# Order of a few steps in a three-layer transformer kernel: where the score banks, row copies, weight splits and gated-attention stages stand in the queues

## The chip, the cores and the metric

The kernel runs on one core of a Trainium2 chip. A core has a matrix engine (TensorE, "PE" in the profile, its weight loads "PEld"), a vector engine (VectorE, "DVE"), an activation engine (ScalarE, "ACT"), GpSimdE ("POOL") and SyncE ("SP", which here only issues DMAs). The engines work their own queues in order and wait for one another by semaphores. The metric is the device time of one execution in microseconds (us), median of three runs.

## The reference, cut to what matters

256 tokens of width 1024 go through two layers of a first block (biased layer norms with modulation from a condition; layer 0 has differential attention, layer 1 multiscale pooling; both have a gated feed-forward) and one layer of a second block (gated linear attention and block attention with a distance bias side by side, then a feed-forward with a squared ReLU). All in float32.

```python
def swiglu(h, w_in, w_out):                     # feed-forward of layers 0 and 1
    g, u = jnp.split(h @ w_in, 2, axis=-1)
    return (jax.nn.silu(g) * u) @ w_out

# first block, end of each layer
x = layer_norm(ALPHA * x + g2 * swiglu(modulate(x, sh2, sc2), ffn_w_in[i], ffn_w_out[i]), ln_g[i, 1], ln_b[i, 1])

# second block
u = rms_norm(x, norm_mix) @ w_in
gq, gk, gv, g_lr, g_r, mq, mk, mv, gate_a, gate_b = jnp.split(u, points, axis=-1)
log_a = jax.nn.log_sigmoid(g_lr @ gla_gate_w2 + gla_gate_b) / GLA_GATE_TAU
o_a = gla_chunked(gq, gk, gv, log_a)            # chunks of 64 tokens, state carried from chunk to chunk
o_a = rms_norm(o_a, gla_out_norm) * jax.nn.silu(g_r)
sc = q @ k.T * scale - slopes * distance        # biased attention, softmax, times mv
y = jax.nn.sigmoid(gate_a) * (o_a @ w_branch_a) + jax.nn.sigmoid(gate_b) * (y_b @ w_branch_b)
x = x + y @ w_out
x = x + jnp.square(jax.nn.relu(rms_norm(x, norm_mlp) @ w_up)) @ w_down
```

## The kernel before

**Tiles.** The 256 tokens are two tiles t of 128. Every large product runs in split float32: an operand x is a rounded high part and a low part (x - high), and a product is three matmuls (high·high, high·low, low·high) in TensorE's fast float32 form. `mmN` (L376 to L378) multiplies tokens by a weight of 512 columns into one PSUM bank, `mmK` (L390, L392) one row block of a weight into two banks, `mmK_tail` (L403 to L405) the last blocks of an output, first half of the columns over all blocks, then the second half.

**Weights.** All weights come as blocks of 128x1024, in the order of a plan written by hand (`make_plan`). Class `Stream` loads them ahead on SP's queue (L255, eleven raw buffers). `emit` takes the next block: a weight is split, high part by ScalarE (L285) and low part by VectorE (L291), into one of eight buffer pairs; a modulation block "m" is a dot product on VectorE (L269). `get(key)` emits until that key is there; `done(keys)` frees a weight's buffers and calls `pump`, which emits up to seven blocks ahead of the last freed one (`R - SLACK`) and one modulation block a call. Where `done` or `get` stands in the program is where the splits stand in the queues of ScalarE and VectorE.

**PSUM.** Eight banks, three rings of two: "big" (two banks each), "mm" and "tr" (one bank each). A ring's next use waits until the use two before it has been read. `tr` serves transposes, `mm` projections, and in the biased attention also the scores.

**The feed-forward of layers 0 and 1** (`ffn`, L942) goes over six chunks j of the inner width: gate and up projections for both tiles, the hook `mid[j]`, then transposes `tr(j, t)` (L981) with their split (L425 on ScalarE into hh, L426 on VectorE into hl), and the output products `o(j - 1, t)` one chunk behind. In the last chunk the order is tr(5,0), o(4,0), tr(5,1), o(5,0), the norm of tile 0, then tile 1. In layer 0 hook 5 is `mid_gbr` (L1095): three calls of `col_row` (L767), which turns a column vector into a row on all partitions by 4 transposes (L774) and a ScalarE copy (L775) for each of two halves, in the tr ring; and `mod_cols` (L858), short VectorE operations on columns that need the modulation blocks. The rows are G and B of the coming norm, and `cur["grow"]`, by which `prescale` (L305) scales the pooling weights.

**The biased attention** (L1315 to L1360) runs between the twelve projections mv0 to gv1: `mo_s` makes scores (L1325, mm ring), bias, maximum and exponential; `mo_t` transposes them (tr ring); `mo_av` multiplies by mv. Two such steps follow each projection from the third on. A projection's result is copied from its bank by ScalarE (mv: L1377), behind the `done` of the weight in tile 1.

**The gated attention** (L1426 to L1507) runs between sixteen further products. Its stages are `g_z` (log gates la, by Abs, Exp and Ln on ScalarE and L1433 on VectorE), `g_b` (sums of la, L1438, and their exponentials), `g_kl` (L1447), `g_qk` (transposes L1455, scaled on VectorE), `g_a`, `g_kv(h)` (L1482, states on VectorE L1487 and L1489) and `g_o(t, h)`; all but g_o use the tr ring. The list `steps` gives one stage after a product, two after products 2 to 5.

**The last feed-forward** goes over eight chunks: `up` (with Relu L1595 on ScalarE and the square L1596 on VectorE), `trm` (transposes L1603), `down`.

Of the kernel before, what the change touches and what calls it, by code (L numbers as in the profile page):

```python
# [13 lines left out]
AF = mybir.ActivationFunctionType  # L14
# [157 lines left out]
def body(ctx: ExitStack, tc: tile.TileContext, wst, prm, cst, cst2, poolp, xT_d, cT_d, x_d, head, lam_d,  # L172
# [769 lines left out]
    def ffn(l, fp, x1_ready, after0, mid1, after1, mid):  # L942
        J = len(FFN_CHUNKS)
        ops_ = None
        hT = {}
        hs = {}

        def gu(j, t, which, ps, mid={}):
            c0, w = FFN_CHUNKS[j]
            n = D * w // (P * BW)  # L950
            lh = xlh(t)
            if is32((which, l, j)):
                lh = lambda k: xf[t, k // 4][:, k % 4]
            mmN(ps[:, :w], lh, mkey((which, l, j), n), width=w, mid=mid)

        def do_g(j, t):
            ps = mmt()
            gu(j, t, "G", ps)
            w = FFN_CHUNKS[j][1]
            h = fp.t([P, 512], f"h{t}", bufs=2)  # L960
            A.activation(h[:, :w], ps[:, :w], AF.Silu)  # L961
            hs[j, t] = h

        def do_u(j, t, mid={}):
            ps = mmt()
            gu(j, t, "U", ps, mid)
            w = FFN_CHUNKS[j][1]
            h = hs[j, t]
            V.tensor_tensor(h[:, :w], h[:, :w], ps[:, :w], op=OP.mult)

        def fin(j, which):
            c0, w = FFN_CHUNKS[j]
            st.done(*mkey((which, l, j), D * w // (P * BW)))

        def tr(j, t):
            w = FFN_CHUNKS[j][1]
            n = w // P
            h = hs.pop((j, t))
            ps = trt()
            for i in range(n):  # L980
                TE.transpose(ps[:, i * P:(i + 1) * P], h[:, i * P:(i + 1) * P], ident)  # L981
            hh = fp.t([P, 4, P], f"hh{t}", F32R, bufs=2)
            hl = fp.t([P, 4, P], f"hl{t}", F32R, bufs=2)
            pv = ps.rearrange("p (k t) -> p k t", t=P)[:, :n]
            split_evac(pv, hh[:, :n], hl[:, :n])
            hT[j, t] = (hh, hl)

        def o(j, t, done):
            n = FFN_CHUNKS[j][1] // P
            hh, hl = hT.pop((j, t))  # L990
            if j == J - 1:
                keys = [("O", l, j, i) for i in range(n)]
                mmK_tail(halves(ops_[t]), [(hh[:, i], hl[:, i]) for i in range(n)], keys)
                if done:
                    st.done(*keys[:HN[l]])
                    st.hold = True
                    st.done(*keys[HN[l]:])
                return
            for i in range(n):
                mmK(halves(ops_[t]), (hh[:, i], hl[:, i]), ("O", l, j, i), j == 0 and i == 0, False)  # L1000
                if done:
                    st.done(("O", l, j, i))

        for j in range(J):
            if j == 0:
                do_g(0, 0)
                do_u(0, 0, {XR[l]: x1_ready})
                if XR[l] == 8:
                    x1_ready()
                do_g(0, 1)  # L1010
                fin(0, "G")
                do_u(0, 1)
                fin(0, "U")
                ops_ = [big(), big()]
            else:
                do_g(j, 0)
                if j == 1:
                    tr(0, 1)
                do_g(j, 1)
                fin(j, "G")  # L1020
                do_u(j, 0)
                do_u(j, 1)
                fin(j, "U")
            if j in mid:
                mid[j]()
            if j < J - 1:
                if j > 0:
                    o(j - 1, 0, False)
                tr(j, 0)
                if j > 0:  # L1030
                    o(j - 1, 1, True)
                    tr(j, 1)
            else:
                tr(j, 0)
                o(j - 1, 0, False)
                tr(j, 1)
                o(j, 0, False)
                if l == 0:
                    for b in range(2):
                        st.prescale(("PW", b))  # L1040
                after0(ops_[0])
                if l == 0:
                    st.hold = True
                o(j - 1, 1, True)
                mid1()
                o(j, 1, True)
                after1(ops_[1])
                if l == 1:
                    st.hold = False
                    st.pump()  # L1050
# [42 lines left out]
        nx["g1p"] = g1p  # L1093

    def mid_gbr():  # L1095
        nx["G"], nx["B"] = col_row(nx["gb"][0]), col_row(nx["gb"][1])
        cur["grow"] = col_row(nx["g1p"])
        nx["cols"] = mod_cols(1, 1, 2)

    mrs = {}  # L1100
    pb = []
# [35 lines left out]
        for f in range(2):  # L1137
            A.activation(pw[t][:, f * 512:(f + 1) * 512], pst[f], AF.Copy)

    ffn(0, fp, x_t(1), ac0(0), mid_pool, ac0(1), {XM: mid_xa, 2: mid_g2c, 3: mid_g2r, 4: mid_gb, 5: mid_gbr})  # L1140


    pps = [big()]
# [171 lines left out]
    def mo_s(t, g):  # L1315
        nh, nk = (4, 128) if t == 0 else (2, 256)
        if g == 0:
            mo_sum[t] = small(8)
        ps = mmt()
        sc = mo.t([P, 512], "sc", bufs=2)  # L1320
        mx = small(4)
        dd = c2c("d0") if t == 0 else c2c("d1")
        for j in range(nh):
            h = nh * g + j
            TE.matmul(ps[:, j * nk:(j + 1) * nk], qT[:, h, t * P:(t + 1) * P], kT2[:, h, 0:nk], start=True, stop=True)  # L1325
        for j in range(nh):
            h = nh * g + j
            sl = slice(j * nk, (j + 1) * nk)
            V.scalar_tensor_tensor(sc[:, sl], dd, 2.0 ** -(h + 1), ps[:, sl], op0=OP.mult, op1=OP.add)
        V.tensor_reduce(mx[:, :nh], sc.rearrange("p (h k) -> p h k", k=nk), AX.X, OP.max, negate=True)  # L1330
        for j in range(nh):
            h = nh * g + j
            sl = slice(j * nk, (j + 1) * nk)
            A.activation(sc[:, sl], sc[:, sl], AF.Exp, bias=mx[:, j:j + 1], accum_out=mo_sum[t][:, h:h + 1])
        mo_st[t, g] = sc
# [36 lines left out]
    seq = [(c, t) for c in ("mv0", "mv1", "gq", "gk", "gv0", "gv1") for t in range(2)]  # L1372
    per = -(-len(steps) // 9)
    for i, (c, t) in enumerate(seq):
        ps = proj(c, t, t == 1)
        if c[:2] == "mv":
            A.activation(mv[:, t, 512 * int(c[2]):512 * int(c[2]) + 512], ps, AF.Copy)  # L1377
        elif c == "gq":
            A.activation(gq[:, t], ps, AF.Copy)
        elif c == "gk":  # L1380
            A.activation(gk[:, t], ps, AF.Copy)
        else:
            A.activation(gv[:, t, 512 * int(c[2]):512 * int(c[2]) + 512], ps, AF.Copy)
        while qk_wait:
            qk_tr()
        if i >= 2:
            for _ in range(per):
                if steps:
                    steps.pop(0)()
# [113 lines left out]
    def g_fin(t):  # L1503
# [5 lines left out]
        for h in range(GH):  # L1509
# [4 lines left out]
    tr_evac(s[1], 1, *obT)  # L1514
    seq = [("gb0", 0), ("gb0", 1), ("gb1", 0), ("gb1", 1), ("bb0", 0), ("bb0", 1), ("bb1", 0), ("bb1", 1),
           ("ga0", 0), ("ga0", 1), ("ga1", 0), ("ga1", 1), ("gr0", 0), ("gr1", 0), ("gr0", 1), ("gr1", 1)]
    steps = [lambda: (g_z(0), g_z(1)), lambda: g_b(0), lambda: g_b(1), lambda: (g_kl(0), g_kl(1)), lambda: g_qk(0), lambda: g_qk(1),
             lambda: g_a(0), lambda: g_a(1), lambda: g_kv(0), lambda: g_kv(1), lambda: (g_o(0, 0), g_o(1, 0)), lambda: g_kv(2),
             lambda: (g_o(0, 1), g_o(1, 1)), lambda: g_kv(3), lambda: (g_o(0, 2), g_o(1, 2)),
             lambda: (g_o(0, 3), g_o(1, 3))]  # L1520

    def oblh(t):
        return lambda k: (obT[0][:, k, t * P:(t + 1) * P], obT[1][:, k, t * P:(t + 1) * P])
# [1 line left out]
    for i, (c, t) in enumerate(seq):  # L1525
# [13 lines left out]
        else:  # L1539
# [5 lines left out]
            else:  # L1545
# [1 line left out]
                A.activation(e, ps, AF.Tanh, scale=0.5)  # L1547
                V.scalar_tensor_tensor(gs[t][:, sl], e, 1.0, ps, op0=OP.add, op1=OP.mult)
                V.tensor_tensor(gs[t][:, sl], gs[t][:, sl], gon[:, sl], op=OP.mult)
        for _ in range(1 + (1 < i < 6)):  # L1550
            if steps:
                steps.pop(0)()
        if (c, t) == ("gr1", 0):
            while steps:
                steps.pop(0)()
            g_fin(0)
    g_fin(1)

# [30 lines left out]
    def up(j, t, mid={}):  # L1589
        ps = mmt()  # L1590
        mmN(ps, xlh(t), mkey(("UP", j), 4), mid=mid)
        if t == 1:
            st.done(*mkey(("UP", j), 4))
        h = fp.t([P, 512], f"h{t}", bufs=2)
        A.activation(h, ps, AF.Relu)  # L1595
        V.tensor_tensor(h, h, h, op=OP.mult)  # L1596
        hs[j, t] = h

    def trm(j, t):
# [30 lines left out]
    for j in range(1, J):  # L1630
        up(j, 0)
        up(j, 1)
        if j < J - 1:
            down(j - 1, 0, False)
            trm(j, 0)
            down(j - 1, 1, True)
            trm(j, 1)
        else:
            trm(j, 0)
            down(j - 1, 0, False)  # L1640
            trm(j, 1)
            down(j, 0, False)
            rcore(0)(ops_[0])
            down(j - 1, 1, True)
            rx_t(0, prmc("nple"))
            down(j, 1, True)
            rcore(1)(ops_[1])
# [122 lines left out]
```

## Time and profile before

| | us |
|---|---|
| median of 3 runs | 1158.18 (1155.91 to 1158.88) |
| the profiled execution | 1158.82 |
| its span, first to last instruction | 1156.8 |
| TensorE / VectorE / ScalarE busy | 1116.0 / 760.6 / 558.8 |

The profile is that of one execution. Its page gives busy shares and the costliest groups of instructions by line; further views of the same trace list who waited for whom, single instructions in order of time, and busy time and granted clock by stretch. A row of a timeline is start, duration, engine, line, operation, output<-inputs by the program's names, forms and count, and in square brackets the idle time before it and who ended it. Rows of several like instructions are merged (x8). Matmuls overlap their neighbours, so distances from start to start say more of TensorE than durations. The granted clock is 1.00 (2.4 GHz) or 0.50 (1.2 GHz).

### The profile page before, as it was taken

How to read it: one execution, taken by the hardware profiler on the slowest of the kernel's cores; microseconds unless marked ns; L12 is line 12 of the kernel's file. 1: busy time of each engine (PE TensorE's matmuls, PEld its weight loads, DVE VectorE, ACT ScalarE, POOL GpSimd, SP SyncE). 2: the span in 40 equal slices, each digit the busy share in tenths (PEclk: the TensorE clock that was granted, in tenths of full speed). 3: DMA queues.
4: the chain of work that ended last, by engine and by line, in shares of the span. 5: the costliest groups of instructions: out<-in, count | busy, mean ns of one | idle time of the engine just before them, and what ended most of it. 6: DMA issues, size and time to landing. Idle time of an engine off the chain costs nothing. (4 is left out here: it accounts for less than half of the span.)

```text
span 1156.8 us, 14163 instructions
## 1 busy us (share of the span) xinstructions
PE 1116.0 (96%) x5186; PEld 881.8 (76%) x5186; DVE 760.6 (66%) x1114; ACT 558.8 (48%) x913; POOL 22.7 (2%) x35
## 2 busy tenths in 40 slices
PE   7999888999999999999999999999999999999998
PEld 3578665678888776888887787886777877888887
DVE  7984967669986875677346765455545785555465
ACT  3452456454444527544444755457235374445353
POOL 0000000000000000000000110000000000000000
PEclk9999989999999999999999999999999999999999
DMA  9972742569997915668563755444344645464611
GB/s 360 351 274 102 273 145 66 196 236 357 354 419 286 336 58 203 218 225 300 170 231 119 241 188 180 146 164 153 102 146 130 216 151 195 166 210 163 206 38 37
DMA packets 65922, 234.62 MB, mean 203 GB/s; under 512 B 7323, under 2 KB 8347, under 8 KB 65852
## 3 DMA queue, kind: packets, MB, share of 16 engines
q1 hardware_dynamic: 64080, 227.97, 55.7%
q10 hardware_dynamic: 1772, 5.74, 1.5%
q8 instruction: 41, 0.67, 0.2%
q14 instruction: 29, 0.24, 0.1%
HBM read 232.63 MB, written 1.05 MB: 202 GB/s over the span
## 5 line engine op out<-in xcount | busy, mean ns | idle before, releaser
L291 DVE TENSOR_TENSOR lo<-raw,hi 128x1024 fp32r<-128x1024 f32 x316 | 375.2, 1220 | 139.8 <-ACT hi L285 136.1
L285 ACT ACTIVATE hi<-raw 128x1024 fp32r<-128x1024 f32 x316 | 322.5, 1056 | 82.9 <-PE mm L378 60.9
L376 PE MATMUL mm<-hi,xTh 128*128 128x512 f32 (+1 forms) x872 | 337.6, 387 | 4.0 <-ACT xTh L425 2.7
L377 PE MATMUL mm<-lo,xTh 128*128 128x512 f32 (+1 forms) x872 | 331.8, 380 | 2.0 <-DVE lo L291 1.3
L378 PE MATMUL mm<-hi,xTl 128*128 128x512 f32 (+1 forms) x872 | 332.2, 381 | 0.6 <-DVE xTl L738 0.4
L376 PEld LDWEIGHTS mm<-hi,xTh 128*128 128x128 f32 x872 | 164.1, 188 | 40.8 <-issue 4.7
L378 PEld LDWEIGHTS mm<-hi,xTl 128*128 128x128 f32 x872 | 164.0, 188 | 34.0 <-DVE xTl L426 1.9
L377 PEld LDWEIGHTS mm<-lo,xTh 128*128 128x128 f32 x872 | 164.2, 188 | 33.5 <-DVE lo L291 3.6
L269 DVE SCALAR_TENSOR_TENSOR raw<-raw,crow 128x1024 f32<-128x1024 f32 x80 | 96.7, 1218 | 0.0
L390 PE MATMUL big<-hi,hh 128*128 128x512 f32 x256 | 80.6, 396 | 0.0
L390 PE MATMUL big<-lo,hh 128*128 128x512 f32 x256 | 79.2, 391 | 0.0
L392 PE MATMUL big<-hi,hl 128*128 128x512 f32 x256 | 79.0, 390 | 0.0
L425 ACT ACTIVATE hh<-tr 128x512 fp32r<-128x512 f32 (+1 forms) x40 | 23.0, 576 | 97.4 <-PE tr L981 54.8
L961 ACT ACTIVATE h<-mm 128x512 f32<-128x512 f32 (+1 forms) x24 | 13.5, 561 | 90.2 <-PE mm L378 90.2
L426 DVE TENSOR_TENSOR hl<-tr,hh 128x512 fp32r<-128x512 f32 (+1 forms) x40 | 26.3, 661 | 46.3 <-ACT hh L425 45.6
L392 PEld LDWEIGHTS big<-hi,hl 128*128 128x128 f32 x256 | 48.1, 188 | 10.4
L390 PEld LDWEIGHTS big<-lo,hh 128*128 128x128 f32 x256 | 48.0, 188 | 10.3
L390 PEld LDWEIGHTS big<-hi,hh 128*128 128x128 f32 x256 | 46.7, 188 | 8.6
L420 POOL TENSOR_TENSOR st<-st,half 128x4 f32<-128x4 f32 (+1 forms) x28 | 21.8, 778 | 1036.8 <-DVE st L418 1023.6
L1596 DVE TENSOR_TENSOR h<-h 128x512 f32<-128x512 f32 x16 | 11.0, 688 | 33.6 <-ACT h L1595 33.5
L1595 ACT ACTIVATE h<-mm 128x512 f32<-128x512 f32 x16 | 9.6, 599 | 38.0 <-PE mm L378 38.0
L667 ACT ACTIVATE p<-big,st 128x512 f32<-128x512 f32 x16 | 11.0, 689 | 31.7 <-DVE st L666 31.7
(316 smaller groups left out, 1261.5 us busy)
## 6 DMA issues: line engine op xcount, KB each, us to landing
raw<-in_dram SPq DMA_DIRECT2D x426, 512.0 KB, 5.0
row<-in_dram ACTq DMA_DIRECT2D x8, 512.0 KB, 6.4
tok<-in_dram SPq DMA_DIRECT2D x8, 256.0 KB, 7.5
xa<-in_dram SPq DMA_DIRECT2D x2, 512.0 KB, 5.7
out_dram<-sg SPq DMA_DIRECT2D x3, 256.0 KB, 2.0
pmat<-in_dram ACTq DMA_DIRECT2D x1, 544.0 KB
crow<-in_dram ACTq DMA_DIRECT2D x1, 512.0 KB, 6.8
out_dram<-sg SPq DMA_DIRECT2D x2, 128.0 KB, 1.7
```

What stands on the lines that cost most here:

```text
L269: V.scalar_tensor_tensor(raw, raw, 1.0, crow, op0=OP.mult, op1=OP.mult, accum_out=mc[l][:, nb:nb + 1])
L285: A.activation(hi, raw, AF.Copy)
L291: V.tensor_tensor(lo, raw, hi.bitcast(F32), op=OP.subtract)
L376: TE.matmul(ps, h, hi[:, sl], start=s, stop=False)
L377: TE.matmul(ps, h, lo[:, sl], start=False, stop=False)
L378: TE.matmul(ps, l, hi[:, sl], start=False, stop=e)
L390: TE.matmul(halves[f], h, w[:, f * 512:(f + 1) * 512], start=first and b == 0, stop=False)
L392: TE.matmul(halves[f], l, hi[:, f * 512:(f + 1) * 512], start=False, stop=last)
L420: G.tensor_tensor(r, v, half_e[:, :w], op=OP.pow)
L425: A.activation(dh, ps, AF.Copy)
L426: V.tensor_tensor(dl, ps, dh.bitcast(F32), op=OP.subtract)
L961: A.activation(h[:, :w], ps[:, :w], AF.Silu)
```

## The change

Six edits of order; no computation is added or left out.

1. `ffn`, last chunk, layer 1: `st.get` of the chunk's last output block stands right behind the transposes of tile 0, where before it was fetched when the product came to it. The same in the last feed-forward for the block ("DN", 7, 3).
2. `ffn`, last chunk: two new hooks, `mid[j, 0]` behind the transposes of tile 0 and `mid[j, 1]` behind o(j - 1, 0). In layer 0 the row B is made in the first and the row for `prescale` in the second; `mid_gbr` keeps G and the columns.
3. The scores of the biased attention take a tr bank and not an mm bank.
4. For mv, `done` in tile 1 stands behind the copy of the bank.
5. The gated attention has eleven steps and not sixteen, one after each of the first eleven products: g_z; g_b of both tiles; g_kl; g_qk(0); g_qk(1); g_a of both; g_kv(0); then for each head both g_o and the next g_kv.
6. The first `up` of tile 1 calls `done` behind Relu and square.

```diff
@@ ffn, last chunk
                 tr(j, 0)
+                if l == 1:
+                    st.get(("O", l, j, FFN_CHUNKS[j][1] // P - 1))
+                if (j, 0) in mid:
+                    mid[j, 0]()
                 o(j - 1, 0, False)
+                if (j, 1) in mid:
+                    mid[j, 1]()
                 tr(j, 1)
                 o(j, 0, False)
@@ hooks of layer 0
     def mid_gbr():
-        nx["G"], nx["B"] = col_row(nx["gb"][0]), col_row(nx["gb"][1])
+        nx["G"] = col_row(nx["gb"][0])
+        nx["cols"] = mod_cols(1, 1, 2)
+
+    def mid_br():
+        nx["B"] = col_row(nx["gb"][1])
+
+    def mid_pr():
         cur["grow"] = col_row(nx["g1p"])
-        nx["cols"] = mod_cols(1, 1, 2)
...
-    ffn(0, ..., {..., 4: mid_gb, 5: mid_gbr})
+    ffn(0, ..., {..., 4: mid_gb, 5: mid_gbr, (5, 0): mid_br, (5, 1): mid_pr})
@@ mo_s
-        ps = mmt()
+        ps = trt()
@@ projections beside the biased attention
-        ps = proj(c, t, t == 1)
-        if c[:2] == "mv":
-            A.activation(mv[:, t, 512 * int(c[2]):512 * int(c[2]) + 512], ps, AF.Copy)
...
+        ps = proj(c, t, t == 1 and c[:2] != "mv")
...
+        A.activation(dst, ps, AF.Copy)
+        if t == 1 and c[:2] == "mv":
+            st.done(*mkey((c,), 4))
@@ steps of the gated attention
-    steps = [lambda: (g_z(0), g_z(1)), lambda: g_b(0), lambda: g_b(1), lambda: (g_kl(0), g_kl(1)), lambda: g_qk(0), lambda: g_qk(1),
-             lambda: g_a(0), lambda: g_a(1), lambda: g_kv(0), lambda: g_kv(1), lambda: (g_o(0, 0), g_o(1, 0)), lambda: g_kv(2),
-             lambda: (g_o(0, 1), g_o(1, 1)), lambda: g_kv(3), lambda: (g_o(0, 2), g_o(1, 2)),
-             lambda: (g_o(0, 3), g_o(1, 3))]
+    steps = [lambda: (g_z(0), g_z(1)), lambda: (g_b(0), g_b(1)), lambda: (g_kl(0), g_kl(1)), lambda: g_qk(0),
+             lambda: g_qk(1), lambda: (g_a(0), g_a(1)), lambda: g_kv(0)]
+    for h in range(GH):
+        def head(h=h):
+            g_o(0, h)
+            g_o(1, h)
+            if h < GH - 1:
+                g_kv(h + 1)
+        steps.append(head)
...
-        for _ in range(1 + (1 < i < 6)):
-            if steps:
-                steps.pop(0)()
+        for f_ in steps[i:i + 1]:
+            f_()
@@ up, last feed-forward
-        if t == 1:
+        if t == 1 and j:
             st.done(*mkey(("UP", j), 4))
         h = fp.t([P, 512], f"h{t}", bufs=2)
         A.activation(h, ps, AF.Relu)
         V.tensor_tensor(h, h, h, op=OP.mult)
+        if t == 1 and not j:
+            st.done(*mkey(("UP", j), 4))
@@ its last chunk
             trm(j, 0)
+            st.get(("DN", j, 3))
             down(j - 1, 0, False)
```

## Rows read from the trace of the kernel before

**Rows 1.** Page, busy us (share of the span), instructions.

```profile
PE 1116.0 (96%) x5186; PEld 881.8 (76%) x5186; DVE 760.6 (66%) x1114; ACT 558.8 (48%) x913; POOL 22.7 (2%) x35
```

**Rows 2.** Waits of TensorE: line, who ended it: us in total, times, longest.

```profile
PE big L404 <- DVE lo L291: 1.8, 3, 0.6
...
PE tr L1603 <- DVE h L1596: 1.3, 1, 1.3
...
PE tr L1447 <- ACT gtmp L1441: 0.9, 2, 0.6
PE tr L1455 <- DVE qkd L1459: 0.8, 1, 0.8
...
PE tr L774 <- ACT row L775: 0.4, 2, 0.3
PE tr L981 <- ACT row L775: 0.4, 2, 0.2
```

**Rows 3.** Timeline of TensorE, end of layer 0's feed-forward (start, us, engine, line).

```profile
392.64 1.03 PE L774 MATMUL tr<-cst,Gc 128*128 128x128 f32 x8
393.92 1.14 PE L774 MATMUL tr<-cst,Bc 128*128 128x128 f32 x8 [0.25 <-ACT row L775]
...
396.60 0.66 PE L981 MATMUL tr<-cst,h 128*128 128x128 f32 x4 [0.20 <-ACT row L775]
...
402.58 0.60 PE L981 MATMUL tr<-cst,h 128*128 128x128 f32 x4
```

**Rows 4.** Timeline of ScalarE in the same stretch.

```profile
393.27 1.09 ACT L775 ACTIVATE row<-tr 128x512 f32<-128x512 f32 x2 [0.39 <-PE tr L774]
```

**Rows 5.** Timeline of VectorE there, first and last of an unbroken run.

```profile
393.44 1.22 DVE L291 TENSOR_TENSOR lo<-raw,hi 128x1024 fp32r<-128x1024 f32 x1
...
402.05 0.68 DVE L426 TENSOR_TENSOR hl<-tr,hh 128x512 fp32r<-128x512 f32 x1
```

**Rows 6.** Timeline of TensorE, two waits that a lower clock followed.

```profile
160.11 1.09 PE L681 MATMUL tr<-cst,p 128*128 128x128 f32 x4 [3.68 <-DVE st L707]
...
823.41 1.55 PE L1482 MATMUL tr<-gv,gk 64*128 64x256 f32 x6 [1.44 <-DVE gst L1489]
```

**Rows 7.** Stretches: us, busy (x) PE, PEld, DVE, ACT, POOL; clock; DMA.

```profile
158.60:165.40 6.80, 5.29 (x20) 3.75 (x20) 4.80 (x11) 5.06 (x15) 0.32 (x1) 0.50 0.68 240
...
824.20:827.50 3.30, 3.30 (x10) 2.17 (x9) 1.39 (x3) 0.00 (x0) 0.00 (x0) 0.50 0.38 151
```

**Rows 8.** Timeline of TensorE, last output blocks of the last feed-forward.

```profile
1112.58 0.39 PE L405 MATMUL big<-hi,hl 128*128 128x512 f32 x1
1112.80 0.39 PE L403 MATMUL big<-hi,hh 128*128 128x512 f32 x1
1113.79 0.50 PE L404 MATMUL big<-lo,hh 128*128 128x512 f32 x1 [0.59 <-DVE lo L291]
```

**Rows 9.** Timeline of ScalarE ahead of it.

```profile
1110.93 0.60 ACT L425 ACTIVATE hh<-tr 128x512 fp32r<-128x512 f32 x1 [5.28 <-PE tr L1603]
```

**Rows 10.** Timeline of TensorE, a projection beside the biased attention.

```profile
717.24 0.50 PE L376 MATMUL mm<-hi,xTh 128*128 128x512 f32 x1 [1.17 <-ACT mv L1377]
```

**Rows 11.** Timeline of ScalarE ahead of it.

```profile
712.82 3.88 ACT L285 ACTIVATE hi<-raw 128x1024 fp32r<-128x1024 f32 x4
716.61 0.57 ACT L1377 ACTIVATE mv<-mm 128x512 f32<-128x512 f32 x1
```

**Rows 12.** Timeline of TensorE, first matmul behind g_b(0).

```profile
790.01 0.48 PE L376 MATMUL mm<-hi,xTh 128*128 128x512 f32 x1
```

**Rows 13.** Timeline of VectorE, la of tile 1.

```profile
790.49 0.69 DVE L1433 SCALAR_TENSOR_TENSOR la<-tr,gtmp 128x512 f32<-128x512 f32 x1 [3.68 <-ACT gtmp L1432]
```

**Rows 14.** Timeline of ScalarE in g_z, first of three table loads.

```profile
784.15 1.28 ACT L1432 ACT_TABLE_LOAD   x1
```

**Rows 15.** Page, groups: out<-in xcount, busy us, mean ns, idle before, releaser.

```profile
L1596 DVE TENSOR_TENSOR h<-h 128x512 f32<-128x512 f32 x16 | 11.0, 688 | 33.6 <-ACT h L1595 33.5
L1595 ACT ACTIVATE h<-mm 128x512 f32<-128x512 f32 x16 | 9.6, 599 | 38.0 <-PE mm L378 38.0
```

More of the change, by code (lines that the diff above doesn't have):

```diff
@@ L1138, in ple @@
             A.activation(pw[t][:, f * 512:(f + 1) * 512], pst[f], AF.Copy)
-    ffn(0, fp, x_t(1), ac0(0), mid_pool, ac0(1), {XM: mid_xa, 2: mid_g2c, 3: mid_g2r, 4: mid_gb, 5: mid_gbr})
+    ffn(0, fp, x_t(1), ac0(0), mid_pool, ac0(1), {XM: mid_xa, 2: mid_g2c, 3: mid_g2r, 4: mid_gb, 5: mid_gbr, (5, 0): mid_br, (5, 1): mid_pr})
     pps = [big()]
@@ L1374, in body @@
     for i, (c, t) in enumerate(seq):
-        ps = proj(c, t, t == 1)
-        if c[:2] == "mv":
-            A.activation(mv[:, t, 512 * int(c[2]):512 * int(c[2]) + 512], ps, AF.Copy)
[L1378 to L1383, printed above, removed]
+        ps = proj(c, t, t == 1 and c[:2] != "mv")
+        dst = dict(mv=mv, gv=gv, gq=gq, gk=gk)[c[:2]][:, t]
+        if c[2:]:
+            dst = dst[:, 512 * int(c[2]):512 * int(c[2]) + 512]
+        A.activation(dst, ps, AF.Copy)
+        if t == 1 and c[:2] == "mv":
+            st.done(*mkey((c,), 4))
         while qk_wait:
@@ L1549, in body @@
                 V.tensor_tensor(gs[t][:, sl], gs[t][:, sl], gon[:, sl], op=OP.mult)
-        for _ in range(1 + (1 < i < 6)):
-            if steps:
-                steps.pop(0)()
+        for f_ in steps[i:i + 1]:
+            f_()
         if (c, t) == ("gr1", 0):
-            while steps:
-                steps.pop(0)()
             g_fin(0)
```

## Prediction

> **What bounds the kernel now.** I read the page's busy shares first: TensorE is busy for 1116.0 of the 1156.8 us of the span [rows 1]. So a change of order is worth what it does to the 40 us in which TensorE stands still, and I went on to the list of TensorE's waits. The waits with names that this change touches are short: 1.8 us in three places for a low part of an output block, 0.9 and 0.8 us in the gated attention, 1.3 us for a squared activation, and 0.4 + 0.4 us for the row copies of the first feed-forward [rows 2]. Then I read the timeline of each place on three engines, to see what a moved step gets in front of it. TensorE, ScalarE and VectorE work their queues in order, so each moved step carries its waits to all that is behind it.
>
> **Row copies between the last blocks of the first feed-forward: a cost.** This edit decides the result. Name the bank uses of the tr ring: before, G1 G2 B1 B2 P1 P2 (two halves of three rows), then T0 = tr(5,0), then o(4,0), then T1 = tr(5,1). The ring has two banks, so each use waits until the one two before it has been read out: B1 starts at 393.92 [rows 3], just after the copy of G1, half of the 1.09 us from 393.27, has ended [rows 4]. After: G1 G2 T0 B1 B2, o(4,0), P1 P2 T1. B2 now takes the bank of T0, and T0's last reader is not ScalarE but VectorE, the subtraction that writes hl. In the trace this hl starts at 402.05 and takes 0.68 us [rows 5]. It can't come sooner in the changed kernel: VectorE runs without a gap from 393.44 to 402.05 [rows 5], four low parts and three modulation dot products of 1.22 us each, which overlap a little, and five short column operations, and all of these were queued by fin(5, "U") and mid_gbr, which still stand ahead of T0. (The columns of mod_cols, moved up within mid_gbr, are those five; their place in VectorE's queue is the same.) In the kernel before nobody minds, since TensorE passes from T0 at 396.60 straight to o(4,0), which fills the time up to T1 at 402.58 [rows 3]. In the changed kernel o(4,0) is queued behind B2, so the cover stands behind the wait.
>
> The sum. Four transposes of a half take about 0.44 us (the copy of G1 starts 0.63 after the first one [rows 3, 4], some 0.2 of it hand-over). T0 starts at 393.92, B1 at about 394.46, when G2's copy has ended, and is through at 394.90. B2 waits until hl ends at 402.73, so it starts at 402.83: TensorE idles for 7.9 us. Then 0.44 for B2, o(4,0) with 402.58 - 396.60 - 0.44 = 5.54 us [rows 3], and P1, P2 and the refill wait of T1, 1.28 us as from G to B now [rows 3]: T1 at 402.83 + 0.44 + 5.54 + 1.28 = 410.09 against 402.58, **+7.5 us**. After it everything keeps its distances to T1, so nothing gives this back: prescale needs P's row, which is copied before T1, and the 0.6 us for the last low part stays, since the early fetch is for layer 1 alone.
>
> To this comes the clock. The trace has a wait of 3.68 us that ends at 160.11 [rows 6], and around it the granted clock is 0.50, the 1.2 GHz level, up to 165.40, that is for 5.3 us after work resumed; after a wait of 1.44 us that ends at 823.41 [rows 6] it is 0.50 for 3.4 us [rows 7]. At half speed half of that time is lost: 2.65 or 1.7 us. A wait of 7.9 us can hardly get less; I take 2.2, between the two. The edit: **+9.7 us** (9.2 to 10.2; 7.5 if the clock stayed up).
>
> **Last output blocks fetched early (layer 1, and the last feed-forward).** In mmK_tail the first half uses all four blocks; the fourth block's low part isn't there, and the matmul at 1112.80 is followed by one at 1113.79, where neighbours stand 0.22 to 0.23 apart [rows 8]: 0.76 us, and 0.1 behind it for the refilled pipeline. Fetched right after the first transposes, the high part on ScalarE and the low part on VectorE go into a stretch in which ScalarE is idle for 5.28 us [rows 9], and the next copy there (hh of the other tile) still finds it done. The fetch moves one raw-block DMA on SP's queue forward too; that queue waits for nothing else here. Twice 0.85: **-1.7 us** (-1.2 to -1.75).
>
> **Scores in the tr banks, value copies ahead of the next splits.** Both aim at one wait. At 717.24 a projection waits 1.17 us [rows 10] for its mm bank, which the copy of mv releases, and this copy, at 716.61, is queued behind four high-part splits of 3.88 us [rows 11]. With the scores out of the mm ring the projection takes a bank that was read one projection earlier; with done behind the copy the copy goes first. Either is enough, so their gains aren't added. Some 0.3 us go beside it, where a projection now waits for a score bank. The four splits of each done move behind the copy, 0.6 us, and the next projection reaches its fourth block some 4 us later, so this is covered. In the tr ring a score bank is refilled by the next scores or transposes only after a projection of 5.5 us, longer than its reading by VectorE; if that cover failed the wait would return under another name. **-1.5 us** (0 to -1.9).
>
> **Gated attention.** Four terms. (1) g_kv(1) no longer follows g_kv(0): the wait that ends at 823.41 [rows 6] goes, 1.5 us, and the 3.4 us at clock 0.50 after it [rows 7], worth 1.7. (2) g_qk(1) gets a projection ahead of it: the wait of 0.8 [rows 2] goes, with the refill 0.95. (3) g_kl after a whole projection: 0.9 [rows 2]. (4) Against it, g_b(1) now comes right after g_b(0), which ends at 790.01 [rows 12], but la of tile 1 is written from 790.49 to 791.18 [rows 13]: a new wait of 1.2 us with the whole next projection queued behind it. Its source, the logarithms and exponentials of g_z on ScalarE, keeps its place. Sum 1.5 + 1.7 + 0.95 + 0.9 - 1.2: **-3.9 us** (-1.5 to -4.5). No later stage has less than a projection between writer and reader.
>
> The three exchanges of tables in g_z cost 1.28 us each by the trace [rows 14]. The Trainium skill (ScalarE: Activation LUTs, section Table sets: the hidden batching unit) says that one set holds both exp and ln, so that they need a single load. By that rule la of tile 1 would come two loads sooner and term (4) would vanish, which is 1.2 us less in the sum, 1159.3; here the trace shows the loads between them, so the row decides.
>
> **Square ahead of done in the last feed-forward.** TensorE waits 1.3 us for the square [rows 2], but Relu (599 ns) and square (688 ns) follow one another whatever stands around them [rows 15]; with only one low part out of the way I take **-0.2 us** (0 to -0.4). The four splits come later by that much and have a projection in front of them.
>
> **How the numbers follow.** +9.7 - 1.7 - 1.5 - 3.9 - 0.2 = +2.4 us. The profiled execution took 1158.82 us (span 1156.8 and 2.0 around it), so 1161.2 by it; that execution is 0.64 above the median of the three runs, 1158.18, so against the median 1160.5. What a measurement of this kernel can tell from no change is about 0.3%, 3.5 us. **Forecast: no change that can be told, 1160.5** (its own range 1158 to 1161.6), the stall in the first feed-forward eating all the other gains: chance 0.61.
>
> **Rivals.** *The clock makes it slower.* The new 1.2 us wait in the gated attention lies between a wait of 1.17 us without a fall of the clock and one of 1.44 with one [rows 10, 6, 7]. If the clock falls there too the 1.7 us of term (1) aren't won, and with 2.65 us lost behind the long wait the sum is +2.4 + 1.7 + 0.45 = +4.6: 1162.7. It decides from the point at which the granted clock shows 0.50 behind g_b. With scores that merely change the name of their wait (the change doing not what it says, +1.5) it is 1164. For it: one fall in the trace followed a wait of 1.44 us; against: the wait at 717 had none. Chance 0.24.
>
> *The row copies are free and it is faster.* If B2's bank were free when it is wanted, the edit would cost nothing and win some of the 0.8 us of row waits, and the other terms would stand: -7.3 to -8, so 1150.5. For it: no row of the kernel before shows a wait of TensorE for hl. Against: hl has seven long operations in front of it in a queue that is worked in order, and the rings' refills are seen to wait for readers on ScalarE and VectorE alike [rows 3, 6]. Chance 0.15, the rest of the doubt about my reading of the queue among it.
>
> From these: faster by over 0.3% 0.15, within 0.3% 0.61, slower by over 0.3% 0.24. The range reaches from 1156 to 1164: the faster case lies outside, the slower one inside.
>
> **What would show it.** In the profile after: transposes of Bc (L774) with an idle time of about 8 us released by VectorE's hl, ahead of o(4,0) at about 403, and a clock of 0.50 behind it; no wait for lo at the tails of layer 1 and of the last feed-forward, one still in layer 0; no wait of a projection for mv; none of g_kv for gst; a new one of about 1.2 us of g_b for la. If the long stall isn't there, the forecast is wrong by its largest term.

## The result: faster by 0.7%, since the long stall wasn't there

The changed kernel takes 1148.99 us (median of four, 1148.72 to 1149.45) against 1157.05 of the kernel before; the ratio is 0.9929, 95% interval 0.9912 to 0.9947. The forecast was 1160.5, no change that can be told. Faster had a chance of 0.15.

The page of the changed kernel has 6 us less of busy TensorE and a span of 1147.2 us [rows 1]:

```profile
span 1147.2 us, 14156 instructions
...
PE 1110.0 (97%) x5186; PEld 880.4 (77%) x5186; DVE 759.9 (66%) x1114; ACT 557.4 (49%) x913; POOL 22.6 (2%) x35
```

Next the list of TensorE's waits in the changed kernel, where it answers [rows 2]: line, who ended it, us in total, times, longest.

```profile
PE tr L1447 <- DVE la L1442: 1.0, 1, 1.0
PE tr L1616 <- DVE h L1607: 1.0, 1, 1.0
PE tr L774 <- ACT row L775: 0.7, 1, 0.7
...
PE big L404 <- DVE lo L291: 0.6, 1, 0.6
PE tr L981 <- ACT row L775: 0.5, 2, 0.3
PE tr L774 <- DVE hl L426: 0.5, 1, 0.5
```

The waits for a low part at an output's last block are down from three to one, that of layer 0; those of g_kv, g_qk, g_kl and of a projection for mv are gone; g_b waits 1.0 us for la, as foreseen. But for hl there is a wait of 0.5 us, and none of 8.

To see what each edit did I took the start of the same matmul in both traces and subtracted, from one mark to the next (us of the two profiled executions):

| stretch of TensorE | before | after | difference | forecast |
|---|---|---|---|---|
| start to the first transpose of G (nothing changed) | 392.64 | 391.54 | -1.10 | 0 |
| from there to the first matmul of o(5,0), layer 0 | 10.30 | 10.99 | **+0.69** | **+9.7** |
| first matmul of o(5,0), layer 1, to the next stage | 18.22 | 17.31 | -0.91 | -0.85 |
| first to last score of the biased attention | 44.15 | 42.32 | -1.83 | -1.5 |
| log-gate projection to g_z | 9.60 | 9.24 | -0.36 | 0 |
| g_z to the transposes behind the gated attention | 105.91 | 100.90 | -5.01 | -3.9 |
| first to second chunk of the last feed-forward | 18.72 | 18.44 | -0.28 | -0.2 |
| tr of its last chunk, tile 1, to the last matmul | 42.18 | 41.28 | -0.90 | -0.85 |

The rows of changed stretches sum to -8.6, which is the measured difference of the medians, -8.1, within the scatter of single executions: up to G, where the kernels are alike, the twelve profiles of this study lie between 390.2 and 393.0. One row isn't the change's: the 0.36 us in front of g_z are scatter, since a second profile of the changed kernel has 9.58 there. Of the changed terms all but two came out within 0.4 us of their forecast; the gated attention won 1.1 us more than forecast, and the one that failed is the largest.

Here is the place, TensorE's timeline of the changed kernel, to be read beside [rows 3]:

```profile
391.54 1.04 PE L774 MATMUL tr<-cst,Gc 128*128 128x128 f32 x8
392.82 0.66 PE L981 MATMUL tr<-cst,h 128*128 128x128 f32 x4 [0.25 <-ACT row L775]
393.31 0.65 PE L774 MATMUL tr<-cst,Bc 128*128 128x128 f32 x4
394.65 0.65 PE L774 MATMUL tr<-cst,Bc 128*128 128x128 f32 x4 [0.69 <-ACT row L775]
400.61 0.60 PE L774 MATMUL tr<-cst,g1p 128*128 128x128 f32 x4
401.69 0.65 PE L774 MATMUL tr<-cst,g1p 128*128 128x128 f32 x4 [0.48 <-DVE hl L426]
402.18 0.60 PE L981 MATMUL tr<-cst,h 128*128 128x128 f32 x4
```

and ScalarE's copy of the first half of B, and VectorE's hl of T0:

```profile
394.01 0.59 ACT L775 ACTIVATE row<-tr 128x512 f32<-128x512 f32 x1
...
400.95 0.68 DVE L426 TENSOR_TENSOR hl<-tr,hh 128x512 fp32r<-128x512 f32 x1
```

hl comes as late as forecast, 400.95 (the same distance behind G as in [rows 5]). But the second half of B starts at 394.65, 0.05 us after the copy of the first half has ended. It took the bank of the first half: that of T0 is still to be read by hl, until 401.63. Only the second half of P waits for hl, at 401.69, when o(4,0) has been done and 0.48 us are left.

### The profile page after: what moved, and what is told of

The parts are those of the page before. It is cut to its first block, busy times and chain, and to the rows that moved or that the text cites. A ratio compares the mean times of both kernels' runs of the same rounds, so it can differ in the third digit from the quotient of the medians.

```text
span 1147.2 us, 14156 instructions
## 1 busy us (share of the span) xinstructions
PE 1110.0 (97%) x5186; PEld 880.4 (77%) x5186; DVE 759.9 (66%) x1114; ACT 557.4 (49%) x913; POOL 22.6 (2%) x35
## 4 chain that ended last, share of the span: by engine, by line
PE 79%; DVE 10%; ACT 4%; issue 3%; DMA 2%; POOL 0%; SPq 0%; ACTq 0%; POOLq 0%; DVEq 0%
PE mm L378 16%; PE mm L376 16%; PE mm L377 16%; PE big L390 12%; PE big L392 6%; DVE lo L291 3%; DMA raw<-in_dram 2%; DVE junkb L526 2%; DVE raw L269 1%; PE big L384 1%; DVE st L666 1%; PE big L404 1%; PE big L405 1%; PE big L403 1%; PE tr L981 1%
```

## The experiments

**Which bank the second half of B takes.** The kernel asks a pool of two for a bank and doesn't say which. If this choice alone made the difference, then the stall of the prediction has to appear as soon as the first half's bank comes free later than T0's. In this kernel VectorE copies the first half, and it does so behind hl.

```diff
     def mid_br():
-        nx["B"] = col_row(nx["gb"][1])
+        r = row()
+        for f in range(2):
+            ps = trt()
...
+            if f == 0:
+                V.tensor_copy(r[:, 0:512], ps)
+            else:
+                A.activation(r[:, 512:1024], ps, AF.Copy)
+        nx["B"] = r
```

> The changed kernel, but the first half of the row B is copied from its bank by VectorE, behind hl, and not by ScalarE; so the second half finds T0's bank as the one that is free first, which is the order of banks that the prediction assumed. Theory 1 (the prediction's arithmetic was right and only the choice of the bank was wrong: in the trace of the changed kernel the second half of B, at 394.65, followed the copy of the first half by 0.05 us, so it had that bank): TensorE stands for 6 to 7 us in front of the second half of B until hl ends at about 401.6, o(4,0) is queued behind it, and the clock falls to 0.50 behind the wait. The first row of o(5,0) moves 6.5 to 7.5 us back without the clock and 8 to 10 with it; the whole is 1156 to 1159. Theory 2 (the cover was there in another way, and a wait of a bank for hl costs next to nothing): within 1 us of the changed kernel, 1149.

Measured: 1157.89 us, ratio 1.0007 to the kernel before (0.9997 to 1.0017): the whole gain is gone. From G to the first matmul of o(5,0) it is 20.14 us, 9.15 more than in the changed kernel and 9.84 more than before. TensorE's timeline (L1111 is the line of B's transposes here), then VectorE's, then stretches (columns as in [rows 7]) of this kernel:

```profile
391.90 0.66 PE L981 MATMUL tr<-cst,h 128*128 128x128 f32 x4 [0.25 <-ACT row L775]
392.40 0.65 PE L1111 MATMUL tr<-cst,Bc 128*128 128x128 f32 x4
400.78 1.11 PE L1111 MATMUL tr<-cst,Bc 128*128 128x128 f32 x4 [7.73 <-DVE hl L426]
409.06 1.04 PE L774 MATMUL tr<-cst,g1p 128*128 128x128 f32 x8
410.34 0.66 PE L981 MATMUL tr<-cst,h 128*128 128x128 f32 x4 [0.25 <-ACT row L775]
...
400.04 0.68 DVE L426 TENSOR_TENSOR hl<-tr,hh 128x512 fp32r<-128x512 f32 x1
...
389.00:395.40 6.40, 3.79 (x24) 2.88 (x22) 5.77 (x9) 2.90 (x5) 0.00 (x0) 1.00 0.99 378
395.60:405.60 10.00, 4.82 (x14) 3.96 (x15) 5.65 (x13) 0.60 (x1) 0.00 (x0) 0.50 0.85 321
405.80:412.00 6.20, 5.95 (x33) 4.84 (x33) 0.33 (x1) 2.05 (x4) 0.00 (x0) 1.00 0.01 3
```

The wait is 7.73 us (forecast 7.9), ended by hl; o(4,0) stands behind it; the clock is 0.50 until about 5 us after work resumed. From the second half of B to P it is 8.28 us, against 0.44 + 5.54 = 5.98 at full clock: the clock costs 2.3 us (forecast 2.2). So the arithmetic of the failed step holds, to 0.15 us of 9.7, for the order of banks that it assumed, and theory 1 stands.

**The edit of the rows undone.** G, B and P ahead of T0 as before, all else changed.

```diff
     def mid_gbr():
-        nx["G"] = col_row(nx["gb"][0])
-        nx["cols"] = mod_cols(1, 1, 2)
+        nx["G"], nx["B"] = col_row(nx["gb"][0]), col_row(nx["gb"][1])
+        cur["grow"] = col_row(nx["g1p"])
+        nx["cols"] = mod_cols(1, 1, 2)
```

> The changed kernel with its second edit undone: G, B and the row for the pooling weights are made one after the other again, ahead of tr(5,0). Theory 1 (with the bank that it got, the edit only exchanges three refill waits of 0.4 us for one of 0.85, one of 0.65 and one of 0.4): 0.6 to 0.8 us faster than the changed kernel, 1148.3, from the first transpose of G to the first matmul of o(5,0) 10.3 us and not 11.0. The prediction's theory (the edit costs 9.7 us): 1139. A third (the edit is what made the kernel faster): 1150 or more.

1148.35 us, ratio 0.9927 (0.9912 to 0.9941). The stretch from G to o(5,0) is 10.39 us, 0.60 less than with the edit. The two whole times can't be told apart, but theory 1 alone gives this stretch. The edit isn't what made the kernel faster; it costs something. How much is less sure than 0.60: where the rows stand as before, this stretch is 10.28 to 10.70 us in six profiles, and 11.0 in both of the changed kernel, so the cost is 0.3 to 0.7 us.

**The gated attention alone**, on the kernel before (the edit stands in the diff above as item 5).

> The kernel before with the new steps of the gated attention alone. Theory 1 (the four terms of the prediction stand: the waits of g_kv, g_qk and g_kl go, with the 3.4 us at clock 0.50, and a wait of 1.2 us of g_b for la comes): 4 to 5.5 us faster than before, 1152 to 1153.5, and a granted clock of 1.00 throughout that part. Rival (the clock's share is no gain, since the new wait of g_b lets it fall as well): 2 to 3 us faster, with a stretch at 0.50 behind g_b.

1152.55 us, ratio 0.996 (0.9946 to 0.9975), 4.7 us less. From g_z to the end of the part it is 100.89 us against 105.91, to 0.01 that of the changed kernel. Three stretches of this run, the clock behind POOL's column:

```profile
760.00:790.00 30.00, 28.99 (x159) 23.50 (x158) 12.88 (x15) 18.91 (x25) 0.61 (x2) 1.00 0.37 132
790.00:820.00 30.00, 30.00 (x146) 24.54 (x145) 20.49 (x32) 17.01 (x21) 0.00 (x0) 1.00 0.62 208
820.00:860.00 40.00, 40.00 (x179) 27.92 (x178) 17.68 (x23) 10.24 (x12) 0.00 (x0) 1.00 0.32 108
```

The new wait of g_b stands in the first of them and did not lower the clock; behind it TensorE is busy throughout. Nor did it in the changed kernel; its row there, and the clock around it:

```profile
787.86 0.82 PE L1447 MATMUL tr<-cst,la 128*128 128x128 f32 x5 [0.98 <-DVE la L1442]
...
785.00:800.00 15.00, 14.02 (x67) 11.03 (x66) 7.84 (x9) 14.24 (x19) 0.00 (x0) 1.00 0.40 140
```

**Scores in tr banks alone, and the copy ahead of done alone**, each on the kernel before.

```diff
-        ps = mmt()
+        ps = trt()
```

> The kernel before with the scores of the biased attention in tr banks, and nothing else. Theory 1 (either of the two edits there removes the one wait of a projection for the copy of mv): the way of TensorE from the first score to the last, 44.15 us before and 42.32 in the changed kernel, is 42.3 to 42.8 us, with no wait for mv or for a score bank. Rival (both edits are needed, since the copy of mv still stands behind four splits and something else waits for it): 43.5 to 44.2. Whole time 1155 to 1156 by theory 1.

From the first score to the last 42.37 us, 1.78 less than before; no wait of a projection for mv is left. The one execution took 1156.28 us.

```diff
-        ps = proj(c, t, t == 1)
+        ps = proj(c, t, t == 1 and c[:2] != "mv")
...
+        A.activation(dst, ps, AF.Copy)
+        if t == 1 and c[:2] == "mv":
+            st.done(*mkey((c,), 4))
```

> The kernel before with the copy of mv ahead of done, and nothing else. Theory 1: the wait for mv goes here too, 42.5 to 42.9 us from the first score to the last, since the waits of 0.2 us of a projection for a score bank stay. Rival: 43.5 to 44.2, the copy is early but the splits are now late for the next projection. Whole time 1155 to 1156 by theory 1.

42.74 us, 1.41 less; the wait for mv is gone, that of 0.2 us for a score bank stays. The one execution took 1156.29 us. Both together had 1.83. Either edit is enough, as the prediction had it; the second adds next to nothing to the first.

This run had a by-catch. Its gated attention is that of before, with the same wait of g_kv, and yet:

```profile
824.00:828.00 4.00, 4.00 (x19) 3.29 (x18) 1.03 (x3) 0.00 (x0) 0.00 (x0) 1.00 0.14 55
```

Its clock stays at 1.00 where it is 0.50 in [rows 7]. Of the four profiles with that order of steps, three show the fall behind the same 1.44 us, one doesn't. From g_z to the end of the part it is 104.35 us without the fall, against 105.91 before: the clock's share of term (1) is 1.6 us, and it is only won where the clock would have fallen. In the run with the scores in tr banks the clock fell once more, behind a wait of only 0.68 us in front of g_z:

```profile
781.30:784.70 3.40, 3.40 (x10) 2.63 (x9) 0.69 (x1) 3.36 (x5) 0.00 (x0) 0.50 0.00 0
```

So its whole time holds a loss that has nothing to do with its edit; the stretch of the scores decides there, not the 1156.28.

**The two early fetches alone**, on the kernel before.

```diff
+                if l == 1:
+                    st.get(("O", l, j, FFN_CHUNKS[j][1] // P - 1))
                 o(j - 1, 0, False)
...
+            st.get(("DN", j, 3))
             down(j - 1, 0, False)
```

> The kernel before with the two early fetches of the last output block alone. Theory 1 (the low part of the fourth block was the only thing that came late): 0.85 to 0.95 us less from the first matmul of each tail to the next stage, no wait of these two places for lo, 1155.3 to 1156.5 in all. Rival (the early splits delay hh or hl of the other tile, so that what is won at the tail is lost behind it): within 0.3 us of before at each place.

One wait of this kind is left of three, that of layer 0:

```profile
PE big L404 <- DVE lo L291: 0.6, 1, 0.6
```

and the two stretches are 0.91 and 0.89 us shorter. The one execution took 1156.47 us. Nothing came back behind them.

**What the remaining waits are worth.** The trace of the changed kernel shows four that a change of order can reach: the rows, the tail of layer 0, g_b's new wait, and one in front of g_z. The first version takes three: the rows stand ahead of T0 again, with B in mm banks; the fetch is made in layer 0 too; and g_b of the two tiles follows two products.

```diff
-                if l == 1:
+                if True:
                     st.get(("O", l, j, FFN_CHUNKS[j][1] // P - 1))
...
+        nx["G"], nx["B"] = col_row(nx["gb"][0]), col_row(nx["gb"][1], bank=mmt)
+        cur["grow"] = col_row(nx["g1p"])
...
-    ... lambda: (g_b(0), g_b(1)), ...
+    ... lambda: g_b(0), lambda: g_b(1), ...
```

> The changed kernel with four further edits: the rows of layer 0 made in one go again, but B in mm banks, which stand idle there; the early fetch of the last output block in layer 0 too; and g_b of the two tiles after two products, so that nothing of g_b waits for la. Theory 1 (each removes a wait that the trace of the changed kernel shows: 1.9 less 0.4 us at the rows, 0.8 at the tail of layer 0, 1.1 in front of g_b): 3 to 3.5 us faster than the changed kernel, 1145.5 to 1146. Rival (these waits cover one another, or the time comes back as a wait for VectorE's low parts in layer 0): 1147.5 to 1149.

1146.9 us, ratio 0.9915 (0.9901 to 0.993). G to o(5,0) is 9.57 us (10.99), the tail of layer 0 is 0.83 shorter, g_z to the end of the gated part 99.63 (100.90): 3.5 us by the stretches, as expected. But the whole time is only 2.1 us below the 1148.99 of the changed kernel, between what theory 1 and the rival expected: two things came back elsewhere. In front of g_z there is a wait again, as in the kernel before; TensorE's row, then VectorE's:

```profile
777.36 1.09 PE L1432 MATMUL tr<-w2b,gst 33*128 33x512 f32 x2 [0.79 <-issue]
...
774.83 0.69 DVE L1405 TENSOR_SCALAR crow<-crow 128x1024 f32<-128x1024 f32 x1 [5.75 <-DMA crow<-in_dram]
```

VectorE had been standing for a DMA, that of the output gains, and hl of the second tile, whose bank g_z needs, is queued behind. The second version scales the gains eight products later:

```diff
-    V.tensor_scalar(gon, gon, 0.5, None, op0=OP.mult)
...
         if c == "ga0" and t == 0:
+            V.tensor_scalar(gon, gon, 0.5, None, op0=OP.mult)
```

> The version with four further edits, and a fifth: the scaling of the output gains of the gated attention stands eight products later on VectorE. In every trace so far VectorE waits 5 to 6 us there for the DMA of these gains, and the wait of g_z behind it was 0.45 us before, 0 in the changed kernel, 0.5 with the rows put back and 0.95 in the version with four edits. Theory 1 (in-order VectorE holds hl of the second tile, and g_z its bank, until that DMA lands): no wait in front of g_z, 0.5 to 0.95 us faster than the version with four edits, 1145.9 to 1146.4; where no clock falls to 0.50 in layer 1's entry as it did once there, 1144.5 to 1145. Rival (the first matmuls of g_z wait for something else): 1146.9.

1146.57 us, ratio 0.9903 (0.9886 to 0.992); g_z follows without a wait,

```profile
776.98 1.55 PE L1431 MATMUL tr<-w2b,gst 33*128 33x512 f32 x3
```

and the stretch before it is 9.24 us in both profiles with this edit, against 10.10. Three of the ten profiles without it have 9.24 too, where the DMA landed sooner, the others 9.37 to 10.10. So what stood in front of g_z was VectorE's queue behind that DMA; in the whole time the 0.3 us of this edit can't be told, and 1146.57 is just outside what was expected.

The other thing that came back is a clock. At the entry of layer 1 a wait of 1.8 us stands in all of these kernels, and in all three profiles of the two versions the clock is 0.50 for 3.4 us behind it, as it is in none of the nine others. From the end of that wait to the first transposes of the last chunk of layer 1 they take 167.95 to 168.20 us, the others 166.55 to 166.60, 1.4 to 1.6 less. The wait and the stretch behind it in the last run below:

```profile
439.66 0.50 PE L376 MATMUL mm<-hi,xTh 128*128 128x512 f32 x1 [1.82 <-ACT xTh L425]
...
440.80:444.10 3.30, 3.30 (x9) 2.53 (x9) 2.15 (x3) 3.27 (x5) 0.00 (x0) 0.50 0.93 325
```

Why just there stays open.

**The changed kernel and the second version on one chip.**

> The changed kernel once more, beside the version with five further edits on the same chip, since the intervals of the two against the kernel before overlap. Theory 1 (the local gains are real): ratio to before 0.993. Rival: the ratio is that of the version with five edits, 0.990.

1150.12 us, ratio 0.993 (0.9917 to 0.9942).

> The version with five further edits beside the changed kernel. Theory 1: its ratio to before is 0.990 to 0.991, 2 to 3 us below the changed kernel, with the intervals apart or nearly so. Rival (what its edits win locally is lost to a clock that falls in layer 1's entry): within 1 us of the changed kernel.

1146.63 us, ratio 0.9902 (0.9887 to 0.9918). The intervals touch, but the slowest of its four executions, 1147.32, is below the fastest of the changed kernel's five, 1148.65: it is faster than both kernels. 3.5 us lie between the medians; by the stretches of the two profiles it is 2.2, 3.8 won and 1.6 lost to the clock. The rest isn't assigned.

## Why the prediction was wrong, point by point

**The step that failed** is the sentence "each use waits until the one two before it has been read out", in the part on the row copies. I took two banks for a strict rotation. The description of PSUM ahead of the prediction says the same, and is wrong with it. They aren't one: in all rows of this case that tell the two apart the next use got the bank whose last reader was through first. With strict turns B2 falls on T0's bank; by this rule it falls on B1's, which ScalarE reads at once. What decides between the two is the changed kernel's own trace: B2 starts at 394.65, 6.3 us before hl begins to read T0's bank. The late_bank run can't tell the rules apart, since both give B2 the bank of T0 there, but it gives the price: it changes only when B1's bank comes free, and the stall of the prediction appears, 7.73 us of it and 2.3 us of clock. So neither the late hl nor the price was wrong; the wait was put on the wrong bank. In place of +9.7 the edit costs +0.69 in this pair of profiles: refill waits of 0.85 at B2, 0.65 at P2 and 0.4 at T0, start to start, for the three of 0.4 before.

**The row that would have told.** The trace of before has it, and I read past it. In g_kv one bank holds the products of chunks 0 and 2, the other that of chunk 1. VectorE reads them so (kernel before):

```profile
822.42 0.42 DVE L1487 COPY gst<-tr 128x256 f32<-128x256 f32 x1
822.88 1.00 DVE L1489 SCALAR_TENSOR_TENSOR gst<-gst,dec,tr 128x256 f32<-128x256 f32 x2
```

Chunk 1 is read first of the two in the second row, until about 823.37, chunk 2 second, until 823.88. By strict turns the next g_kv begins in the bank of chunks 0 and 2, at 823.9 at the earliest. It began at 823.41 [rows 6], in the bank that came free first. I had used that row for the clock and not asked which bank it was.

**The other terms.** The fetches: -0.91 and -0.90 for -0.85 each; right, with their cover, the idle ScalarE, and a little past the end of their range. Scores and copy: -1.83 for -1.5; either is enough, shown by both alone. The gated attention: -5.01 for -3.9, outside its range of -1.5 to -4.5. Its four terms are in the traces; start to start, from the kernel before to the one with the new steps alone, g_kv gives 1.60 (forecast 1.5) and its clock 1.57 (1.7), g_qk 1.24 (0.95), g_kl 1.55 (0.9), and the new wait of g_b costs 1.30 (1.2). I had taken the listed idle time for g_kl and little more for g_qk, and a wait costs more than that from start to start: the listed 1.44 of g_kv is 1.60. The rest, 0.36, lies in the products between the stages. The square: -0.28 for -0.2. The forecast of the log-gate part was none, and rightly: the 0.36 us there came by a DMA that landed a little sooner relative to the work, and the second profile of the changed kernel doesn't have them.

**The rivals.** The faster one was the right outcome, and close in its number, 1150.5, but not by its reason: the bank wasn't free when it was wanted; it was another bank. Its number is luck in part, too: it let the row edit win up to 0.7 us where it cost some, and the gated attention made up for that. I gave it 0.15 because I took the rotation for known when only one refill in the rows, B1, had been compared with it, and B1 fits both rules. The slower one, a clock that falls behind g_b, isn't seen in any of the five profiles that have that wait.

**The rule on tables of the Trainium skill** (ScalarE: Activation LUTs, section Table sets: the hidden batching unit) says that one load serves exp and ln. It was weighed rightly as a rule that this trace doesn't follow: three loads of 1.28 us are there in g_z of the changed kernel as well, and g_b waits for la.

## What to carry to other kernels

A pool of two banks was no rotation here: before a stall is charged to a refill, find out which bank the use got, from a row where two readers of a pair end at different times, or from the allocation itself. A long forecast that hangs on one such assignment deserves the largest doubt, however well the rest is worked out. And a step moved in front of covered work is as dear as its latest reader: one copy on the other engine made the stretch 9.15 us longer here.

## What the runs showed of the chip

The granted clock behind a given wait isn't fixed. Behind the same wait of 1.44 us in front of g_kv it was 0.50 for 3.4 us in three profiles and 1.00 in a fourth; in front of g_z it was 0.50 for 3.4 us behind 0.68 us once, and 1.00 behind 0.79 us in the first version; behind the 0.9 to 1.0 us of g_b it never fell in five profiles, and behind the 1.82 us at the entry of layer 1 it fell in three of twelve; behind the 7.73 us it was 0.50 for 10.2 us in all, half of that after work had resumed, and cost 2.3 us. A term of a sum that is clock should be given with a chance, not as a number.
